# Up products of an MLP by pairs of weight blocks, in seven block products instead of eight, with the square of the norm's rate applied on the down products

## The chip, the cores and the metric

The kernel runs on one core of one Trainium2 chip. The metric is the device time of one execution in microseconds. Matrix products run on TensorE (PE in the profile; the loading of weights is the row PEld), element-wise work on VectorE (DVE), ScalarE (ACT) and GpSimd (POOL), and transfers are issued by SyncE (SP). All of these take their instructions in order from queues of their own and meet at semaphores.

## The reference

Two layers of a streaming encoder over 640 positions (512 of a prompt, 8 x 16 of samples), 1024 features, all in float32. The change concerns the last line of a layer:

```python
def trunk_layer(x, ...):
    h = rmsnorm(x, ln1)
    proj = h @ w_in                                  # all branches
    ...
    x = x + mix @ w_o
    h2 = rmsnorm(x, ln2)
    x = x + jnp.square(jax.nn.relu(h2 @ w_up)) @ w_down   # w_up 1024 x 4096, w_down 4096 x 1024
```

rmsnorm multiplies each position by a rate 1/sqrt(mean(x^2) + 1e-6) and each feature by a weight. The rate is positive, so relu(rate * y)^2 = rate^2 * relu(y)^2, and a factor for each position can be applied before or after any product over features.

## The kernel before

Activations lie feature by feature: `x` is 128 partitions x 8 chunks x 640 positions. Every float32 matrix operand is kept as two float32r parts, hi (a copy on ACT, rounded) and lo (the difference, on DVE), made by `split`. A product takes three matmuls for each chunk of 128 features: hi times hi, hi times lo, lo times hi (`three`). The 640 positions go in two halves of 320 columns, so one block of 128 output features (`gemm`) is 2 halves x 8 chunks x 3 = 48 matmuls of 128x128 by 128x320. Its result is a `pair`: one PSUM tile of two banks, one for each half (pg_up, pg_dn, pg_wo in the profile); there are two such pairs in turn. There are also two single banks `c` and two `d`.

Weights come in blocks of 128x1024 in the order of a list (`Feed`): `load` issues the transfer of one block (three buffers raw), `ahead` splits the next block into whi and wlo (two buffers of each) and loads another, and `take` hands out the split block and asks for the one after it. The splits are set ahead of other work by a priority; a scheduler orders ACT, DVE, POOL and SP by priorities, and the order of PE is the order of the source (`manual_schedule`).

The MLP of a layer (`mlp`) has 32 up blocks and 32 down blocks, in four groups b of eight. All eight up blocks of group 0 come first; then, for each b, two up blocks of the next group, the eight down blocks of b, and the other six up blocks. After an up block, `relu2` takes relu and the rate out of the pair on DVE, squares it to the hi part on ACT and again on POOL, and takes the lo part on DVE: 128x640 each. After a down block DVE adds the pair to `x`. The last eight down blocks are in `residual`, which also sums the squares for the next norm. Ahead of the MLP `residual_raw` makes the products with w_o (pg_wo), adds them to `x` and splits x times the norm's weight into Ah and Al, without the rate; the rate follows beside the first up block. Its last block is taken half by half (`halves=True`): DVE reads the first half of the pair while the second is still to be multiplied.

## Time and profile before

| | |
|---|---|
| median of the runs shown | 2523.02 us (lowest 2522.17) |
| the profiled execution's own time | 2522.23 us |
| its span | 2520.5 us |
| PE busy | 2465.8 us, 98% of the span, 18456 matmuls |
| DVE, ACT, POOL busy | 1300.5, 1024.0, 564.8 us |
| DMA | 104 GB/s in the mean |
| up products, both layers | 3 x 1024 matmuls |
| down products, both layers | 3 x 1024 matmuls |

The page gives busy time by engine, then by forty slices of the span, then groups of instructions with the mean time of one and the idle time ahead of them. The mean of a matmul is from its start to its end; matmuls overlap, so the time from one start to the next is shorter and is read from rows in order of time.

### The profile page before, as it was taken

What the parts mean: (1) busy time and instruction counts of PE and PEld (TensorE: products, weight loads), DVE (VectorE), ACT (ScalarE), POOL (GpSimd) and SP (SyncE); (2) the same over time, 40 slices, a digit from 0 to 9 for tenths busy, and PEclk for the clock granted to TensorE, in tenths of its full rate; (3) what the DMA queues carried; (4) which work ended last, traced back from release to release, by engine and by line L of the source; (5) the groups of instructions that cost most, each with busy time, mean ns of one, the idle gap of its engine ahead of it and who ended that gap; (6) DMA issues with size and microseconds to landing.
All of it is one profiled execution on the core that took longest, in us unless ns stands there. A gap on an engine that the chain in (4) does not pass through costs nothing. (4 is left out here: it accounts for less than half of the span.)

```text
span 2520.5 us, 45083 instructions
## 1 busy us (share of the span) xinstructions
PE 2465.8 (98%) x18456; PEld 2386.6 (95%) x18456; DVE 1300.5 (52%) x2686; ACT 1024.0 (41%) x1968; POOL 564.8 (22%) x638
## 2 busy tenths in 40 slices
PE   8999999999999999999999999999999999999998
PEld 7999999998999999999999999999989999999997
DVE  6656776537555433333445677664275653333333
ACT  5766666533223212122346666774332222122122
POOL 0234433211222201011213333331112221011012
PEclk9999999999999999999999999999999999999999
DMA  5224333336532222222233333333565222222221
GB/s 176 91 96 129 95 95 94 118 118 243 166 102 67 76 76 76 76 76 76 76 98 111 100 95 95 100 120 112 156 213 149 90 70 76 76 74 75 74 73 67
DMA packets 124494, 261.28 MB, mean 104 GB/s; under 512 B 17233, under 2 KB 57073, under 8 KB 124289
## 3 DMA queue, kind: packets, MB, share of 16 engines
q1 hardware_dynamic: 123968, 257.10, 32.2%
q8 instruction: 145, 2.38, 0.4%
q0 software_dynamic: 320, 1.31, 0.2%
q14 instruction: 61, 0.49, 0.1%
HBM read 218.22 MB, written 40.15 MB: 103 GB/s over the span
## 5 line engine op out<-in xcount | busy, mean ns | idle before, releaser
L133 ACT ACTIVATE whi<-raw 128x1024 fp32r<-128x1024 f32 x304 | 321.8, 1059 | 1022.0 <-issue 359.9
L134 DVE TENSOR_TENSOR wlo<-raw,whi 128x1024 fp32r<-128x1024 f32 x304 | 397.3, 1307 | 164.0 <-ACT whi L133 155.6
L80 PE MATMUL pg_dn<-gl,whi 128*128 128x320 f32 x1024 | 316.6, 309 | 2.1 <-DVE gl L1111 2.1
L80 PE MATMUL pg_up<-Ah,whi 128*128 128x320 f32 x1024 | 317.1, 310 | 0.0
L80 PE MATMUL pg_dn<-gh,whi 128*128 128x320 f32 x1024 | 316.7, 309 | 0.0
L80 PE MATMUL pg_up<-Ah,wlo 128*128 128x320 f32 x1024 | 316.4, 309 | 0.0
L80 PE MATMUL pg_dn<-gh,wlo 128*128 128x320 f32 x1024 | 316.4, 309 | 0.0
L80 PE MATMUL pg_up<-Al,whi 128*128 128x320 f32 x1024 | 316.4, 309 | 0.0
L80 PE MATMUL pg_g<-Ah,whi 128*128 128x320 f32 x896 | 289.6, 323 | 0.0
L80 PE MATMUL pg_g<-Ah,wlo 128*128 128x320 f32 x896 | 276.8, 309 | 0.0
L80 PE MATMUL pg_g<-Al,whi 128*128 128x320 f32 x896 | 276.4, 308 | 0.0
L1110 POOL TENSOR_TENSOR r<-r 128x640 f32<-128x640 f32 x64 | 101.8, 1591 | 684.8 <-ACT gh L1109 684.8
L80 PE MATMUL pg_p<-Ah,whi 128*128 128x320 f32 x768 | 252.8, 329 | 0.0
L80 PE MATMUL pg_p<-Al,whi 128*128 128x320 f32 x768 | 237.4, 309 | 0.4 <-DVE Al L134 0.4
L80 PE MATMUL pg_p<-Ah,wlo 128*128 128x320 f32 x768 | 237.6, 309 | 0.0
L80 PEld LDWEIGHTS pg_dn<-gl,whi 128*128 128x128 f32 x1024 | 192.2, 188 | 2.6 <-DVE gl L1111 2.6
L80 PEld LDWEIGHTS pg_up<-Ah,whi 128*128 128x128 f32 x1024 | 192.2, 188 | 0.0
L80 PEld LDWEIGHTS pg_up<-Al,whi 128*128 128x128 f32 x1024 | 192.2, 188 | 0.0
L80 PEld LDWEIGHTS pg_dn<-gh,whi 128*128 128x128 f32 x1024 | 192.2, 188 | 0.0
L80 PEld LDWEIGHTS pg_dn<-gh,wlo 128*128 128x128 f32 x1024 | 192.2, 188 | 0.0
L80 PEld LDWEIGHTS pg_up<-Ah,wlo 128*128 128x128 f32 x1024 | 192.2, 188 | 0.0
L80 PEld LDWEIGHTS pg_g<-Ah,whi 128*128 128x128 f32 x896 | 168.6, 188 | 7.8 <-issue 3.5
(689 smaller groups left out, 5386.8 us busy)
## 6 DMA issues: line engine op xcount, KB each, us to landing
raw<-in_wblk SPq DMA_DIRECT2D x304, 512.0 KB, 3.6
gd<-sg SPq DMA_DIRECT2D x56, 320.0 KB, 3.5
rg<-gd SPq DMA_DIRECT2D x44, 320.0 KB, 3.3
S<-in_sdelta SPq DMA_DIRECT2D x16, 512.0 KB, 6.1
out<-S SPq DMA_DIRECT2D x16, 512.0 KB, 3.6
gr<-rowd SPq DMA_DIRECT2D x16, 320.0 KB, 4.9
er<-rowd SPq DMA_DIRECT2D x16, 320.0 KB, 4.0
ond<-osb SPq DMA_DIRECT2D x16, 320.0 KB, 2.2
```

The source lines that it names most:

```text
L80: nc.tensor.matmul(out, lhsT=lhsT, rhs=rhs, start=start, stop=stop, **kw)
L133: nc.scalar.activation(dst_hi, src, AF.Copy)
L134: nc.vector.tensor_tensor(dst_lo, src, dst_hi.bitcast(F32), op=ALU.subtract)
L1110: nc.gpsimd.tensor_tensor(r[:], r[:], r[:], op=ALU.mult)
```

## The change

In each layer the first four up blocks stay as they were, except that relu is taken on ACT and the rate is left out. The other 28 are done two at a time by `seven(b, m)`. The pair's weights are cut into four parts of 128x512 (two halves of the input features times two blocks), the activations into four of 4 chunks x 320 positions. Winograd's form of Strassen's scheme takes seven products of such parts, of 12 matmuls each, instead of eight. In the order of PE they are called P1 to P7 here:

| | result | weights | activations |
|---|---|---|---|
| P1 | Z, new | first half of block m | Ah, Al, first features, first positions |
| P2 | Y, new | second half of block m | second features, first positions |
| P3 | Z, added | t1, first half | S2 |
| P4 | X, new | t1, second half | S1 |
| P5 | Z, added | t2, first half | S3 (written over a quarter of Ah, Al) |
| P6 | X, added | second half of block m+1 | S4 |
| P7 | Z, added | t2, second half | second features, second positions |

Z and X are the two banks of one pair (pg_zx), Y is a single bank `c`. Between products ACT copies what Z holds after P1 (z1) and after P3 (z2) and X after P4 (x5); DVE adds Y and z1, Z and x5 (after P5), X and z2 (after P6). Relu, the two squares and the lo part follow from these sums, all on ACT and DVE. The weight sums t1 and t2 are made on DVE from the raw blocks, and each of the weights wa (block m), wb (t1), wc (half of t2, half of block m+1) and wd (half of t2) is split on ACT and DVE into the two buffers of whi and wlo in turn. S1 to S4 are made once for each layer, from x times the norm's weight, on ACT and DVE beside the four single up blocks. A down block's sum is now two instructions on DVE: the pair times the square of the rate, and the addition to `x`.

```diff
         def parts(self, pl):
-            raw = self.raw.pop(0)
+            self.last = self.raw.pop(0)
+            return self.of(pl, self.last[:])
+        def of(self, pl, *src):
...
             hi = pl.tile([P, D], F32R, tag="whi", bufs=2, name="whi")
             lo = pl.tile([P, D], F32R, tag="wlo", bufs=2, name="wlo")
+            at = 0
             with tc.high_priority(offset=AHEAD):
-                split(hi[:], lo[:], raw[:])
+                for v in src:
+                    n = v.shape[-1]
+                    split(hi[:, at:at + n], lo[:, at:at + n], v)
+                    at += n
             return hi, lo
...
-            nc.scalar.activation(u, pr[:, 0:HT], AF.Copy)
+            nc.scalar.activation(u, pr[:, 0:HT], AF.Copy if self.power == 1 else AF.Square)
...
         def add(xs, ps, dst, first):
-            nc.vector.tensor_tensor(xs, ps[:, :, 0:HT], xs, op=ALU.add)
+            plus(xs, ps, dst)
             nrm.add(dst, xs, first, nc.vector if dst == 1 else nc.gpsimd)
...
+            def flat(nm, rows):
+                return pl.tile([P, rows, HT], F32, tag="r", bufs=3, name=f"{nm}{l}")
+            def squares(r, hi, lo, eng):
+                nc.scalar.activation(hi, r, AF.Square)
+                if eng is None:
+                    nc.scalar.activation(r, r, AF.Square)
+                else:
+                    eng.tensor_tensor(r, r, r, op=ALU.mult)
+                nc.vector.tensor_tensor(lo, r, hi.bitcast(F32), op=ALU.subtract)
             def relu2(ps, hi, lo):
-                r = pl.tile([P, 2, HT], F32, tag="r", bufs=3, name=f"r{l}")
-                nc.vector.scalar_tensor_tensor(r[:], ps[:, :, 0:HT], 0.0, v2(nrm.r[:]), op0=ALU.max, op1=ALU.mult)
-                nc.scalar.activation(hi, r[:], AF.Square)
-                nc.gpsimd.tensor_tensor(r[:], r[:], r[:], op=ALU.mult)
-                nc.vector.tensor_tensor(lo, r[:], hi.bitcast(F32), op=ALU.subtract)
+                r = flat("r", 2)
+                nc.scalar.activation(r[:], ps[:, :, 0:HT], AF.Relu)
+                squares(r[:], hi, lo, nc.gpsimd)
             def up(b, ms):
                 for m in ms:
                     hi, lo = (v2(v[:, m % 2, :]) for v in dst(b, m))
                     run(gemm(l, WB_UP + b * KC + m, Ah, Al, f"up{l}{b}{m}", lambda ps: relu2(ps, hi, lo)), rates)
-            up(0, range(KC))
+            A = {(k, a): [v[:, 4 * k:4 * k + 4, half[a]] for v in (Ah, Al)] for k in range(2) for a in range(2)}
+            S = {i: [psum_pool.tile([P, 4, HT], F32R, name=f"S{i}{t}{l}")[:] for t in "hl"] for i in (1, 2, 4)}
+            S[3] = A[0, 1]
+            tmp = [pl.tile([P, 4, HT], F32, tag=t, name=f"s{i}{l}")[:] for i, t in enumerate(("gh", "gl", "gh", "gl", "gh"))]
+            def scaled(d, k, a):
+                for i in range(4):
+                    c = nrm.c0 + 4 * k + i
+                    nc.scalar.activation(d[:, i, :], x[:, 4 * k + i, half[a]], AF.Copy, scale=col[:, c:c + 1])
+            def plus(d, s0, s1):
+                nc.vector.tensor_tensor(d, s0, s1, op=ALU.add)
+            q, p, sm, u, v = tmp
+            up(0, range(2))
+            scaled(q, 1, 1)
+            scaled(p, 0, 1)
+            plus(sm, p, q)
+            split(*S[1], sm)
+            up(0, range(2, 3))
+            scaled(u, 0, 0)
+            plus(sm, sm, u)
+            split(*S[2], sm)
+            plus(p, p, u)
+            scaled(v, 1, 0)
+            plus(sm, sm, v)
+            split(*S[4], sm)
+            up(0, range(3, 4))
+            split(*S[3], p)
+            stacks.pop().close()
+            pw = ExitStack()
+            stacks.append(pw)
+            pt = pw.enter_context(phase(f"nt{l}", side="right"))
+            def seven(b, m):
+                gh, gl = dst(b, m)
+                wa = feed.take(l, WB_UP + b * KC + m, ahead=False)
+                B = {}
+                for i, raw in enumerate((feed.last, feed.raw.pop(0))):
+                    B[0, i], B[1, i] = raw[:, 0:512], raw[:, 512:1024]
+                s1, s2 = (pt.tile([P, 2, 512], F32, tag=t, name=f"{t}{l}{b}{m}") for t in ("t1", "t2"))
+                with tc.high_priority(offset=AHEAD):
+                    sub = lambda d, s0, y: nc.vector.tensor_tensor(d, s0, y, op=ALU.subtract)
+                    neg = lambda d, s0, y: nc.vector.scalar_tensor_tensor(d, s0, -1.0, y, op0=ALU.mult, op1=ALU.subtract)
+                    sub(s1[:, 1, :], B[0, 0], B[0, 1])
+                    neg(s1[:, 0, :], s1[:, 1, :], B[1, 1])
+                wb = feed.of(wp, s1[:].rearrange("p a b -> p (a b)"))
+                zx, y = pair(f"zx{l}{b}{m}"), bank("c", f"y{l}{b}{m}")
+                Z, X, Y = zx[:, 0, 0:HT], zx[:, 1, 0:HT], y[:, 0:HT]
+                def product(ps, w, i, act, first):
+                    hi, lo = (t[:, 512 * i:512 * i + 512].rearrange("p (k c) -> p k c", k=4) for t in w)
+                    ah, al = act
+                    for k in range(4):
+                        for j, (wt, act) in enumerate(((hi, ah), (hi, al), (lo, ah))):
+                            nc.tensor.matmul(ps, lhsT=wt[:, k, :], rhs=act[:, k, :], start=first and k + j == 0,
+                                             stop=k == 3 and j == 2, skip_group_check=True)
+                def copy(t, ps):
+                    c = pt.tile([P, HT], F32, tag=t, name=f"{t}{l}{b}{m}")
+                    nc.scalar.activation(c[:], ps, AF.Copy)
+                    return c[:]
+                def add(d, ps, c):
+                    nc.vector.tensor_tensor(d, ps, c, op=ALU.add)
+                product(Z, wa, 0, A[0, 0], True)
+                z1 = copy("z1", Z)
+                product(Y, wa, 1, A[1, 0], True)
+                r0, r1 = flat("ra", 2), flat("rb", 2)
+                add(r0[:, 0, :], Y, z1)
+                with tc.high_priority(offset=AHEAD):
+                    sub(s2[:, 0, :], B[1, 1], B[0, 1])
+                    neg(s2[:, 1, :], s1[:, 0, :], B[1, 0])
+                wc = feed.of(wp, s2[:, 0, :], B[1, 1])
+                feed.load()
+                product(Z, wb, 0, S[2], False)
+                z2 = copy("z2", Z)
+                product(X, wb, 1, S[1], True)
+                x5 = copy("x5", X)
+                wd = feed.of(wp, s2[:, 1, :])
+                product(Z, wc, 0, S[3], False)
+                with tc.high_priority(offset=AHEAD):
+                    add(r1[:, 1, :], Z, x5)
+                product(X, wc, 1, S[4], False)
+                add(r0[:, 1, :], X, z2)
+                nc.scalar.activation(r0[:], r0[:], AF.Relu)
+                squares(r0[:], gh[:, :, half[0]], gl[:, :, half[0]], None)
+                feed.ahead()
+                product(Z, wd, 0, A[1, 1], False)
+                nc.scalar.activation(r1[:, 0, :], Z, AF.Relu, scale=-1.0)
+                nc.scalar.activation(r1[:, 1, :], r1[:, 1, :], AF.Relu, scale=-1.0)
+                squares(r1[:], gh[:, :, half[1]], gl[:, :, half[1]], None)
+            def plus_products(xs, ps, a):
+                t = flat("t", 2)
+                rate = v2(nrm.r[:]) if a is None else rep(nrm.r[:, half[a]], 1, 2)
+                nc.vector.tensor_tensor(t[:], ps[:, :, 0:HT], rate, op=ALU.mult)
+                nc.vector.tensor_tensor(xs, t[:], xs, op=ALU.add)
+            seven(0, 4)
+            seven(0, 6)
             for b in range(FF // D):
                 if b + 1 < FF // D:
-                    up(b + 1, range(2))
+                    seven(b + 1, 0)
                 gh, gl = Chunks(tiles, b, 0), Chunks(tiles, b, 1)
                 if b + 1 == FF // D:
                     last = l + 1 == DEPTH
-                    es.close()
-                    es = ExitStack()
+                    stacks.pop().close()
+                    stacks.pop().close()
+                    es = stacks.pop()
                     pn = es.enter_context(phase(f"na{l}", side="right"))
-                    return es.close, residual(l, WB_DN + b * KC, gh, gl, f"dn{l}", Norm(pn, 32 if last else 16 * (l + 1), f"a{l}", last))
+                    return es.close, residual(l, WB_DN + b * KC, gh, gl, f"dn{l}", Norm(pn, 32 if last else 16 * (l + 1), f"a{l}", last), plus_products)
                 for m in range(KC):
-                    def add(ps):
-                        nc.vector.tensor_tensor(v2(x[:, m, :]), ps[:, :, 0:HT], v2(x[:, m, :]), op=ALU.add)
-                    run(gemm(l, WB_DN + b * KC + m, gh, gl, f"dn{l}{b}{m}", add))
-                up(b + 1, range(2, KC))
+                    run(gemm(l, WB_DN + b * KC + m, gh, gl, f"dn{l}{b}{m}", lambda ps: plus_products(v2(x[:, m, :]), ps, None)))
+                for m in (2, 4, 6):
+                    seven(b + 1, m)
```

Three places in the order of the built programs follow. The first is TensorE in layer 0, group 1, blocks 4 and 5. Before, at the border of the two halves of block 4 (what is awaited stands behind a row; Activation_49 and DVE_49 are the semaphores that ACT and DVE count up, PE_49 that of PE):

```order
L80 MATMUL pg_up014_10252<-Ah_98,whi_10184 128x320
L80 MATMUL pg_up014_10252<-Al_99,whi_10184 128x320
L80 MATMUL pg_up014_10252<-Ah_98,wlo_10185 128x320
L80 MATMUL pg_up014_10252<-Ah_98,whi_10184 128x320
L80 MATMUL pg_up014_10252<-Al_99,whi_10184 128x320
L80 MATMUL pg_up014_10252<-Ah_98,wlo_10185 128x320
```

TensorE now, the last rows of P3 and the first of P4:

```order
L1198 MATMUL pg_zx014_10375<-S2h0_9044,whi_10371 128x320
L1198 MATMUL pg_zx014_10375<-S2l0_9045,whi_10371 128x320
L1198 MATMUL pg_zx014_10375<-S2h0_9044,wlo_10372 128x320
L1198 MATMUL pg_zx014_10375<-S1h0_9042,whi_10371 128x320 [waits Activation_49]
L1198 MATMUL pg_zx014_10375<-S1l0_9043,whi_10371 128x320
```

Where P3 wrote Z and P4 begins X, in the other bank, a wait has come in. TensorE now, the last rows of P5 and the first of P6:

```order
L1198 MATMUL pg_zx014_10375<-Ah_98,whi_10408 128x320
L1198 MATMUL pg_zx014_10375<-Al_99,whi_10408 128x320
L1198 MATMUL pg_zx014_10375<-Ah_98,wlo_10409 128x320
L1198 MATMUL pg_zx014_10375<-S4h0_9046,whi_10408 128x320 [waits DVE_49]
L1198 MATMUL pg_zx014_10375<-S4l0_9047,whi_10408 128x320
```

The halves of an up block follow each other without a wait, while a product on one bank of pg_zx stands behind a wait for ACT (by its count, the copy z2) or for DVE (by its count, the sum of Z and x5). P5 in the same way waits for the copy x5 and P7 for the sum of X and z2, in all 28 pairs.

The second place is ScalarE. Before, at up blocks of group 0 (the row of two kinds in turn is the same in all groups):

```order
L133 ACTIVATE whi_9248<-raw_0_92_9130 128x1024 [waits DMAHW4_49,PE_49,Activation_49]
L1109 ACTIVATE gh002_9186<-r0_9243 128x640 [waits DVE_49]
L133 ACTIVATE whi_9310<-raw_0_93_9192 128x1024 [waits DMAHW5_49,PE_49,Activation_49]
L1109 ACTIVATE gh002_9186<-r0_9303 128x640 [waits DVE_49]
L133 ACTIVATE whi_9370<-raw_0_94_9252 128x1024 [waits DMAHW6_49,PE_49,Activation_49]
L1109 ACTIVATE gh004_9308<-r0_9365 128x640 [waits DVE_49]
```

ScalarE now, at the pair of blocks 4 and 5 of group 1 (z1, z2 and x5 are the copies, whi_10408 is wc, whi_10444 wd):

```order
L1203 ACTIVATE z1014_10389<-pg_zx014_10375 128x320 [waits PE_49]
L1123 ACTIVATE gh012_10229<-rb0_10268 128x2x320 [waits Activation_49]
L1125 ACTIVATE rb0_10268<-rb0_10268 128x640 [waits Activation_49]
L133 ACTIVATE whi_10408<-t2014_10368 128x512 [waits DVE_49,PE_49]
L133 ACTIVATE whi_10408<-raw_0_101_10278 128x512 [waits DMAHW5_49]
L1203 ACTIVATE z2014_10428<-pg_zx014_10375 128x320 [waits PE_49]
L133 ACTIVATE whi_10444<-t2014_10368 128x512 [waits DVE_49,PE_49]
L1203 ACTIVATE x5014_10442<-pg_zx014_10375 128x320 [waits PE_49]
```

Two kinds of rows in turn have become a list in which copies out of PSUM stand between splits of weights.

The third place is ScalarE at the first pair of layer 0 (blocks 4 and 5 of group 0), where the rows before are those shown above, and where now S2, S3 and S4 are still being made:

```order
L133 ACTIVATE S2h0_9044<-s20_9050 128x1280 [waits DVE_49]
L133 ACTIVATE whi_9363<-t1004_9359 128x1024 [waits PE_49]
L1132 ACTIVATE r0_9346<-pg_up003_9297 128x640 [waits PE_49,Pool_49]
L133 ACTIVATE Ah_98<-s10_9049 128x4x320 [waits DVE_49]
L1123 ACTIVATE gh002_9214<-r0_9346 128x640 [waits Activation_49]
L133 ACTIVATE whi_9400<-t2004_9360 128x512 [waits PE_49]
L133 ACTIVATE whi_9400<-raw_0_93_9220 128x512 [waits DMAHW5_49]
L133 ACTIVATE S4h0_9046<-s20_9050 128x1280 [waits DVE_49]
L1203 ACTIVATE z1004_9381<-pg_zx004_9367 128x320
```

Here the copy z1, for which P3 waits, stands behind wc (whi_9400), whose buffer is free after P2, and behind the hi part of S4. Layer 1 has the same order.

More of the change, by code (lines that the diff above doesn't have):

```diff
@@ L280, in encoder, with __init__ @@
     class Norm:
-        def __init__(self, pl, c0, nm, final=False, whole=False):
-            self.pl, self.c0, self.nm, self.final = pl, c0, nm, final
-            self.r = pl.tile([P, NT], F32, tag="rate", name=f"rate{nm}") if whole else None
+        def __init__(self, pl, c0, nm, final=False, whole=None, power=1):
+            self.pl, self.c0, self.nm, self.final, self.power = pl, c0, nm, final, power
+            self.r = whole.tile([P, NT], F32, tag="rate", name=f"rate{nm}") if whole else None
             self.acc = pl.tile([P, 2, HT], F32, tag="acc", name=f"acc{nm}")
@@ L833, in heads @@
             else:
-                nrm = Norm(pf, 0, "a", whole=True)
+                nrm = Norm(pf, 0, "a", whole=pf)
                 Rh = pf.tile([P, KC, NT], F32R, name="Rh")
@@ L1050, in merge, with residual @@
                         run(gemm(l, WB_PA + m, Ah, Al, f"pa{l}{m}", pa))
-            es = ExitStack()
-            nrm = Norm(es.enter_context(phase(f"nb{l}", side="right")), 8 * (2 * l + 1), f"b{l}", whole=True)
-            return es, nrm, residual_raw(l, WB_WO, Bh, Bl, f"wo{l}", nrm)
-    def residual(l, b0, ah, al, nm, nrm):
+            stacks = [ExitStack() for _ in range(3)]
+            pr, ps, pn = (es.enter_context(phase(f"n{nm}{l}", side="right")) for es, nm in zip(stacks, "rsb"))
+            nrm = Norm(pn, 8 * (2 * l + 1), f"b{l}", whole=pr, power=2)
+            return stacks, ps, nrm, residual_raw(l, WB_WO, Bh, Bl, f"wo{l}", nrm)
+    def residual(l, b0, ah, al, nm, nrm, plus):
         def add(xs, ps, dst, first):
-            nc.vector.tensor_tensor(xs, ps[:, :, 0:HT], xs, op=ALU.add)
+            plus(xs, ps, dst)
             nrm.add(dst, xs, first, nc.vector if dst == 1 else nc.gpsimd)
@@ L1094, in residual_raw, with mlp @@
         return rates()
-    def mlp(l, es, nrm, rates):
+    def mlp(l, stacks, psum_pool, nrm, rates):
         with phase(f"mlp{l}", 5) as pl:
@@ L1124, in mlp @@
                     last = l + 1 == DEPTH
-                    es.close()
-                    es = ExitStack()
+                    stacks.pop().close()
+                    stacks.pop().close()
+                    es = stacks.pop()
                     pn = es.enter_context(phase(f"na{l}", side="right"))
-                    return es.close, residual(l, WB_DN + b * KC, gh, gl, f"dn{l}", Norm(pn, 32 if last else 16 * (l + 1), f"a{l}", last))
+                    return es.close, residual(l, WB_DN + b * KC, gh, gl, f"dn{l}", Norm(pn, 32 if last else 16 * (l + 1), f"a{l}", last), plus_products)
                 for m in range(KC):
-                    def add(ps):
-                        nc.vector.tensor_tensor(v2(x[:, m, :]), ps[:, :, 0:HT], v2(x[:, m, :]), op=ALU.add)
-                    run(gemm(l, WB_DN + b * KC + m, gh, gl, f"dn{l}{b}{m}", add))
-                up(b + 1, range(2, KC))
+                    run(gemm(l, WB_DN + b * KC + m, gh, gl, f"dn{l}{b}{m}", lambda ps: plus_products(v2(x[:, m, :]), ps, None)))
+                for m in (2, 4, 6):
+                    seven(b + 1, m)
     ctx.enter_context(tc.manual_schedule(engines={mybir.EngineType.PE}))
```

## The prediction

> **What bounds the kernel now.** I read the page's shares of engines first, then the windows of the MLP, then the groups by shape, then the rows in order of time around one up block, and last the waits of TensorE.
>
> ```profile
> span 2520.5 us, 45083 instructions
> PE 2465.8 (98%) x18456; PEld 2386.6 (95%) x18456; DVE 1300.5 (52%) x2686; ACT 1024.0 (41%) x1968; POOL 564.8 (22%) x638
> ```
>
> The windows of layer 0 (columns: length, then busy us and instructions of PE, PEld, DVE, ACT, POOL, then granted clock, DMA share, GB/s), with the start of the kernel and the products with w_o for comparison:
>
> ```profile
> 20.00:30.00 10.00, 8.25 (x38) 7.85 (x39) 6.08 (x14) 4.06 (x6) 0.33 (x1) 0.66 0.23 71
> 730.00:800.00 70.00, 67.48 (x457) 66.73 (x456) 42.68 (x40) 21.26 (x28) 17.59 (x9) 1.00 0.25 76
> 800.00:820.00 20.00, 19.05 (x136) 18.79 (x135) 8.43 (x14) 6.04 (x9) 3.29 (x3) 1.00 0.17 53
> 870.00:1230.00 360.00, 358.94 (x2447) 358.68 (x2446) 125.29 (x129) 74.27 (x82) 42.27 (x27) 1.00 0.25 77
> ```
>
> In the MLP (last row) TensorE has 2447 matmuls in 360 us and no idle time; DVE is busy for 35%, ACT for 21%, transfers for 25%. So a matmul fewer is worth what lies between two starts, and any wait that TensorE meets there is paid in full.
>
> Rows of time at the end of one up block and the start of the next:
>
> ```profile
> 818.52 0.82 DVE L1108 SCALAR_TENSOR_TENSOR r<-pg_up,rateb 128x640 f32<-128x640 f32 x1 [2.89 <-PE pg_up L80]
> ...
> 825.07 0.31 PE L80 MATMUL pg_up<-Al,whi 128*128 128x320 f32 x1
> 825.22 0.31 PE L80 MATMUL pg_up<-Ah,wlo 128*128 128x320 f32 x1
> ...
> 825.46 1.06 ACT L133 ACTIVATE whi<-raw 128x1024 fp32r<-128x1024 f32 x1 [5.34 <-issue]
> ...
> 825.56 0.82 DVE L1108 SCALAR_TENSOR_TENSOR r<-pg_up,rateb 128x640 f32<-128x640 f32 x1 [2.85 <-PE pg_up L80]
> ```
>
> A matmul lasts 0.31 us but the next starts 0.15 us later: from one DVE row to the next are 7.04 us, and a block has 48 matmuls, so 0.1467 us is the price of one. Two delays are read here as well. DVE begins on the result 0.34 us after the block's last matmul began (825.22 to 825.56). ACT overwrites a whi buffer 0.24 us after that same start; the matmul before it was the last to read the buffer.
>
> **Part 1, the matmuls removed.** A pair of blocks has 7 x 12 = 84 matmuls instead of 96: 12 x 0.1467 = 1.76 us. There are 14 pairs in each layer, 28 in all: 28 x 1.76 = -49.3 us. If nothing waited, a pair would take 12.32 us in place of 14.08.
>
> **Part 2, the waits inside a pair.** P4, P5, P6 and P7 each begin with a wait on an instruction that reads the other bank, and that instruction itself waits for the end of the product just before. TensorE has nothing to do in between, since its order is fixed. The trace has one place of this form: the last pg_wo block, half by half, where DVE reads the first half before TensorE begins the second.
>
> ```profile
> 794.09 2.19 DVE L134 TENSOR_TENSOR Al<-hwo,Ah 128x640 fp32r<-128x640 f32 x1
> ...
> 794.80 0.31 PE L80 MATMUL pg_wo<-Bh,wlo 128*128 128x320 f32 x1
> 796.20 0.48 DVE L1076 TENSOR_TENSOR x<-pg_wo,x 128x320 f32<-128x320 f32 x1
> ...
> 796.73 0.41 PE L80 MATMUL pg_wo<-Bh,whi 128*128 128x320 f32 x1 [1.62 <-DVE x L1076]
> ...
> 796.99 0.30 PE L80 MATMUL pg_wo<-Bl,whi 128*128 128x320 f32 x1
> ...
> 797.12 0.31 PE L80 MATMUL pg_wo<-Bh,wlo 128*128 128x320 f32 x1
> ...
> 800.40 1.06 ACT L133 ACTIVATE whi<-raw 128x1024 fp32r<-128x1024 f32 x1 [2.80 <-PE pg_wo L80]
> ...
> 801.37 0.45 ACT L292 ACTIVATE sqb<-x 128x320 f32<-128x320 f32 x1
> ```
>
> TensorE starts 0.05 us after DVE has ended (796.68 to 796.73), and the next start comes 0.26 us later instead of 0.15: a restart costs 0.11 us. DVE was late here for a reason of its own (the 2.19 us row); without it the wait would be 0.34 + 0.48 + 0.05. The last two rows show that a queued ACT instruction starts 0.09 us before the one ahead has ended.
>
> Durations by shape (busy us and mean ns of one):
>
> ```profile
> L133 ACT ACTIVATE whi<-raw 128x1024 fp32r<-128x1024 f32 x304 | 321.8, 1059 | 1022.0 <-issue 359.9 <-PE pg_dn L80 256.3 <-PE pg_up L80 79.1
> ...
> L134 DVE TENSOR_TENSOR wlo<-raw,whi 128x1024 fp32r<-128x1024 f32 x304 | 397.3, 1307 | 164.0 <-ACT whi L133 155.6
> ...
> L1110 POOL TENSOR_TENSOR r<-r 128x640 f32<-128x640 f32 x64 | 101.8, 1591 | 684.8 <-ACT gh L1109 684.8
> ...
> L1109 ACT ACTIVATE gh<-r 128x640 fp32r<-128x640 f32 x64 | 46.9, 732 | 0.0
> ...
> L1131 DVE TENSOR_TENSOR x<-pg_dn,x 128x640 f32<-128x640 f32 x48 | 39.6, 825 | 221.3 <-PE pg_dn L80 221.3
> ...
> L821 ACT ACTIVATE sg<-pg_g 128x640 f32<-128x640 f32 x56 | 39.2, 700 | 13.4 <-DMA gd<-sg 12.9
> ...
> L461 ACT ACTIVATE cb<-pg_p 128x320 f32<-128x320 f32 x48 | 20.1, 419 | 0.0
> ...
> L343 ACT ACTIVATE ha<-x,col 128x320 f32<-128x320 f32 x32 | 16.2, 550 | 3.7 <-DMA out<-ha 3.3 <-DVE Al L134 0.4
> ```
>
> The copies z1, z2 and x5 are 128x320 out of PSUM on ACT, as cb<-pg_p is: 0.42 us. The sums are 128x320 on DVE, as the row at 796.20 is: 0.48 us. A 128x512 split is not shown; half of 128x1024 is 0.53 us and the whole 1.06, and on the line through the 320-wide (0.45, the row at 801.37) and the 1024-wide row it would be 0.62, which I take. Each wait is counted from the start of the last matmul of the product ahead, less the 0.147 us that the next would have come later anyhow:
>
> - P4 waits for z2: 0.34 + 0.42 + 0.05 - 0.15 = 0.66.
> - P5 waits for x5, which stands on ACT behind the hi split of wd, and that waits for P4's last reads of wb's buffer: 0.24 + 0.62 - 0.09 + 0.42 + 0.05 - 0.15 = 1.09.
> - P6 waits for DVE's sum of Z and x5: 0.34 + 0.48 + 0.05 - 0.15 = 0.72.
> - P7 waits for DVE's sum of X and z2: 0.72.
>
> These are 3.19 us, and four restarts 0.44: 3.63 us in a pair, against 1.76 saved. The net is +1.87, a pair takes 15.95 us, and 28 x 1.87 = +52.4 us. From below, without restarts and with x5 ahead of the split, it is 2.76 - 1.76 = +1.0; from above, with half a microsecond more for a queue that is late once, +2.4: 28 to 66 us.
>
> P1 and P3 are taken at nothing in a steady pair. P2 covers the copy z1 (0.34 + 0.42 against 1.76). For P1 of the next pair the whole split wa must follow P5 (the wc buffer) and stand ready after P6 and P7, which are 1.76 us each and now have waits beside them: 1.06 on ACT and 1.31 on DVE, of which the two overlap only in part, leave some 0.4 us. If that cover goes, each pair pays for it; that is the second rival.
>
> What hides the rest: in a pair ACT has 3 copies, splits of 1024, 1024, 3 x 512, relu and squares of two halves, about 9.7 us of 16, and DVE, by the rows above with half of 1.31 for each 512-wide one, about 10.6 of 16. Both have more than before in a pair but neither is full, and nothing on TensorE waits for gh and gl until their group's down blocks. POOL loses its squares there. The two raw transfers of a pair keep their time of 14 to 16 us, twice what a block's split had. A down block's sum has one more 0.83 us row on DVE beside 7.04 us of products, which only the last one doesn't hide.
>
> **Part 3, the first pair of each layer.** Here z1 stands on ACT behind the making of S1 to S4. From the end of the second single up block until z1 is done, ACT has the hi split of that stretch's weights twice (2 x 1.06), relu and square twice (2 x 1.43), eight scaled copies (8 x 0.55), three splits of 1280 columns (about 1.28 each by the same line), wc (2 x 0.62) and z1 (0.42): 14.9 us, less some 1.5 for the overlaps (0.09 each), plus about 0.8 for DVE's sums between them: 14.2. TensorE needs it after 72 matmuls, 10.56 us. The wait at P3 is about 3.7 us, twice: +7.4 (0 to 12).
>
> That idle time has its own consequence. The only idle time of that order of size among long runs of matmuls is at the start:
>
> ```profile
> PE pg_gf L80 <- ACT whi L133: 2.6, 1, 2.6
> PE pg_wo L80 <- DVE x L1076: 3.2, 2, 1.6
> PE pg_dn L80 <- DVE gl L1111: 2.1, 2, 1.1
> ```
>
> ```profile
> 18.43 0.31 PE L80 MATMUL pg_gf<-Rh,wlo 128*128 128x320 f32 x1
> ...
> 21.39 0.63 PE L80 MATMUL pg_gf<-Rh,whi 128*128 128x320 f32 x1 [2.65 <-ACT whi L133]
> ...
> 27.08 0.47 PE L80 MATMUL pg_gf<-Rh,whi 128*128 128x320 f32 x1
> 27.35 0.46 PE L80 MATMUL pg_gf<-Rl,whi 128*128 128x320 f32 x1
> 27.61 0.34 PE L80 MATMUL pg_gf<-Rh,wlo 128*128 128x320 f32 x1
> ```
>
> After 2.65 us of idle time the starts are 0.27 us apart, until 27.6 us, and the window 20:30 has a clock of 0.66. Its 38 matmuls would take 5.6 us and took 8.6 less 0.4 of another wait: about 2.7 us lost. After the 1.6 us wait in pg_wo the clock stayed 1.00. A 3.7 us wait may bring the loss in both layers or in neither; I take it once: +2.7 (0 to 5.4).
>
> [...]
>
> **Part 4, the ends.** The last down block's sum stands ahead of the final norm, and has a second DVE instruction: +0.8. The waits of pg_dn for gl (2.1 us in both layers) come from a last up block whose lo part is late; POOL's 1.6 us square is gone there, and I take -1.2 (-2.1 to 0).
>
> **Sum.** -49.3 + 101.6 (28 x 3.63) + 7.4 + 2.7 + 0.8 - 1.2 = +62.0 us against the profiled execution's 2522.2: 2584 us. The median is 2523.02, and the forecast is 2.4% above it. The bounds of the terms: lowest 28 + 0 + 0 + 0.8 - 2.1 = +27, highest 66 + 12 + 5.4 + 0.8 = +84, so 2549 to 2606.
>
> **The rivals.**
>
> The other side: *the border waits are cheap*. The place is P4 to P7. If TensorE begins while the other bank is read, the four cost nothing and the time is 2522.2 - 49.3 + 9.7 = 2483 us, no slower than before. It decides where a border costs under (49.3 - 9.7) / 112 = 0.35 us in the mean. For it: the two banks hold different results, and nothing computed by P4 needs z2. Against: the 1.62 us row shows TensorE waiting in just such a case, and the built program has the wait. Even a copy that lasted nothing would leave 0.34 + 0.05 - 0.15 + 0.11 = 0.35. Chance 0.05. [...] A part of the waits (z2 and x5 hidden, the two sums paid: 2 x 0.83 a pair) would give 2522.2 - 49.3 + 46.5 + 9.7 = 2529; chance 0.05.
>
> *The queues pile up.* At the turn of a pair, ACT has relu, two squares and wa's split, and DVE two lo parts, wa's lo split and the next sums. If a square or a lo part (0.73 to 0.83) comes ahead of what TensorE waits for, twice in a pair, it costs about 1.5 us: 28 x 1.5 = 42, 2584 + 42 = 2626. For it: the margin of 0.4 us at P1. Against: the splits and the P6 sum are put ahead by priority, and both engines have 5 us free in a pair. Chance 0.13.
>
> *The clock halves within pairs.* TensorE is now idle for 3.2 of 16 us. If this brings one loss of 2.7 us in each pair: 28 x 2.7 = 76, 2660. For it: the row of 2.65 us. Against: 1.62 us left the clock at 1.00, and no wait in a steady pair is above 1.1. Chance 0.07. [...]
>
> **How the numbers follow.** The forecast has 0.70, and the rivals 0.05, 0.05, 0.13 and 0.07. The range takes in the forecast's bounds and the queues up to 2630: 2549 to 2630; what is left out are the two cheap cases, the clock and a little of the queues, about 2 in 10. A measurement of this kernel tells about 2% from no change: 2472.6 and 2573.5. The forecast's own 2549 to 2606 lies to three quarters above 2573.5, so slower has 0.70 x 0.75 + 0.13 + 0.07 = 0.72; the rest of it and the cheap cases are within 2%, 0.26; faster by over 2% would need more than all matmuls saved at no cost, 0.02.
>
> **What would show it.** Right: TensorE has 336 matmuls fewer; four rows of idle time in a pair, of about 0.6 to 0.8 us and one of 1.1, ended by z2, x5 and the two sums; starts of Z's first products 16 us apart; one wait of 3 to 4 us for z1 in each layer; the clock at 1.00 in the pairs. Wrong: waits below 0.35 us, or pairs 14 us or less apart; a wait at P1 or P3 in each pair; clock below 1.00 in the windows of pairs; or idle time that moved into the down blocks.

## The result, and the profile after

The changed kernel takes 2588.32 us (median, 2585.98 to 2591.85), against 2523.64 us for the kernel before on the same chip: a ratio of 1.0264, with a 95% interval from 1.0247 to 1.028. It is slower by 2.6%; the forecast was 2584 us, 2.4%, in a range from 2549 to 2630.

The first lines of the page after:

```profile
span 2585.7 us, 44993 instructions
PE 2450.6 (95%) x18120; PEld 2340.2 (91%) x18120; DVE 1477.5 (57%) x2982; ACT 1213.4 (47%) x2324; POOL 476.9 (18%) x582
```

TensorE has the 336 matmuls fewer (18456 to 18120) and is busy for 15 us less, but the span is 65 us longer. TensorE's share falls from 98% to 95%, and the waits of TensorE (awaited instruction: us in total, times, longest) say for what:

```profile
PE pg_zx L1198 <- ACT x L1203: 25.1, 28, 0.9
PE pg_zx L1198 <- ACT z L1203: 21.2, 30, 3.2
PE pg_zx L1198 <- DVE rb L1207: 18.2, 28, 0.7
PE pg_zx L1198 <- DVE ra L1207: 16.4, 28, 0.6
...
PE pg_dn L80 <- DVE gl L1128: 0.4, 2, 0.2
```

The four lines on pg_zx are new. x is the copy x5 (P5 waits), z is z2 in 28 pairs and z1 twice, rb is the sum of Z and x5 (P6), ra that of X and z2 (P7). Rows in order of time through one steady pair, with the start of P5 in the pair before for the period (rows left out are marked by dots):

```profile
985.54 0.41 PE L1198 MATMUL pg_zx<-Ah,whi 128*128 128x320 f32 x1 [0.90 <-ACT x L1203]
...
998.17 0.44 ACT L1203 ACTIVATE z<-pg_zx 128x320 f32<-128x320 f32 x1 [0.65 <-PE pg_zx L1198]
...
998.66 0.41 PE L1198 MATMUL pg_zx<-S1h,whi 128*128 128x320 f32 x1 [0.53 <-ACT z L1203]
...
1000.58 0.63 ACT L133 ACTIVATE whi<-t 128x512 fp32r<-128x512 f32 x1 [1.97 <-PE pg_zx L1198]
1001.11 0.42 ACT L1203 ACTIVATE x<-pg_zx 128x320 f32<-128x320 f32 x1
...
1001.59 0.41 PE L1198 MATMUL pg_zx<-Ah,whi 128*128 128x320 f32 x1 [0.90 <-ACT x L1203]
...
1003.70 0.49 DVE L1207 TENSOR_TENSOR rb<-pg_zx,x 128x320 f32<-128x320 f32 x1 [1.77 <-PE pg_zx L1198]
...
1004.25 0.42 PE L1198 MATMUL pg_zx<-S4h,whi 128*128 128x320 f32 x1 [0.64 <-DVE rb L1207]
...
1006.22 1.06 ACT L133 ACTIVATE whi<-raw 128x1024 fp32r<-128x1024 f32 x1 [1.52 <-PE pg_zx L1198]
1006.32 0.49 DVE L1207 TENSOR_TENSOR ra<-pg_zx,z 128x320 f32<-128x320 f32 x1 [2.13 <-PE pg_zx L1198]
...
1006.87 0.42 PE L1198 MATMUL pg_zx<-Ah,whi 128*128 128x320 f32 x1 [0.58 <-DVE ra L1207]
...
1007.31 1.23 DVE L134 TENSOR_TENSOR wlo<-raw,whi 128x1024 fp32r<-128x1024 f32 x1 [0.50 <-ACT whi L133]
...
1009.02 0.31 PE L80 MATMUL pg_dn<-gh,wlo 128*128 128x320 f32 x1
```

Each PE row with a bracket is the first matmul of P4, P5, P6 or P7, and just ahead of it ends the copy or sum that reads the other bank. The last two rows, the lo split of the next weights and the first matmul that reads it, are taken up further below. From P5 to P5 of the next pair (985.54 to 1001.59) are 16.05 us, where 14.08 were taken before and 12.32 would be without waits.

The windows at the first pair of each layer and at steady pairs (last columns: granted clock, DMA share, GB/s):

```profile
840.00:850.00 10.00, 6.42 (x31) 5.76 (x32) 9.07 (x12) 3.49 (x7) 1.43 (x1) 0.83 0.17 52
1000.00:1030.00 30.00, 27.88 (x187) 27.09 (x186) 11.26 (x13) 9.57 (x14) 0.00 (x0) 1.00 0.28 88
2120.00:2130.00 10.00, 7.47 (x45) 6.69 (x46) 8.41 (x12) 2.26 (x6) 0.00 (x0) 1.00 0.19 54
```

The clock is 1.00 in the steady pairs. It fell in layer 0 at the first pair (0.50 from 842.43 to 845.85 us) and not in layer 1, though the wait for z1 was 3.21 us in both.

To compare kernels below I use the stretch of one MLP, from the start of its first pg_up matmul to that of its last pg_dn matmul in the trace, since the rest of the kernel, in which no run changed more than the last sum, differs by some microseconds from one profiled execution to the next (between the two MLPs 784 to 791 us). That difference goes with the granted clock: by the clock records of the traces it was at 0.50 there for 3 x 3.4 us in the kernel before, the change and x5dve (789.3 to 791.1 us), and not at all in banks, early and halves2 (783.9 to 784.7); over the whole executions the mean granted clock was 0.993 to 0.994 in the first three and 0.995 to 0.996 in the others.

| kernel | time, us | kernel before beside it | ratio (95%) | MLP of layer 0, of layer 1, us |
|---|---|---|---|---|
| before | | | | 457.0, 456.9 |
| the change | 2588.32 | 2523.64 | 1.0264 (1.0247 to 1.028) | 488.9, 487.5 |
| banks | 2495.73 | 2521.37 | 0.9902 (0.9884 to 0.992) | 444.5, 444.3 |
| x5dve | 2581.66 | 2521.37 | 1.0241 (1.0226 to 1.0257) | 485.7, 484.8 |
| z1first | 2587.22 | 2521.37 | 1.0259 (1.0242 to 1.0276) | 492.2, 487.2 |
| early | 2579.38 | 2522.66 | 1.0223 (1.0206 to 1.0241) | 486.0, 485.9 |
| halves | 2607.67 | 2521.37 | 1.0346 (1.033 to 1.0361) | 500.1, 500.2 |
| rateonly | 2524.17 | 2522.66 | 1.0011 (1.0 to 1.0022) | 457.7, 457.7 |
| halves2 | 2575.02 | 2522.66 | 1.0205 (1.019 to 1.022) | 483.4, 483.4 |
| best | 2480.76 | 2522.66 | 0.9837 (0.9818 to 0.9856) | 437.7, 437.6 |
| best2 | 2476.37 | 2520.25 | 0.9824 (0.9806 to 0.9843) | 434.1, 434.5 |

Of the 65 us by which the span grew, 31.9 + 30.6 = 62.5 lie in the two MLPs.

### The profile page after: what moved, and what is told of

Read it like the earlier page. It is cut to its first block, busy times and chain, and to the rows that moved or that the text cites. A ratio compares the mean times of both kernels' runs of the same rounds, so it can differ in the third digit from the quotient of the medians.

```text
span 2585.7 us, 44993 instructions
## 1 busy us (share of the span) xinstructions
PE 2450.6 (95%) x18120; PEld 2340.2 (91%) x18120; DVE 1477.5 (57%) x2982; ACT 1213.4 (47%) x2324; POOL 476.9 (18%) x582
## 5 line engine op out<-in xcount | busy, mean ns | idle before, releaser
L133 ACT ACTIVATE whi<-raw 128x1024 fp32r<-128x1024 f32 (+1 forms) x304 | 309.0, 1018 | 686.1 <-PE pg_dn L80 256.6
L134 DVE TENSOR_TENSOR wlo<-raw,whi 128x1024 fp32r<-128x1024 f32 (+1 forms) x304 | 383.5, 1263 | 170.1 <-ACT whi L133 167.9
L80 PEld LDWEIGHTS pg_g<-Al,whi 128*128 128x128 f32 x896 | 168.7, 188 | 1.5
L1241 DVE TENSOR_TENSOR t<-pg_dn,rateb 128x640 f32<-128x640 f32 x64 | 52.7, 824 | 205.0 <-PE pg_dn L80 205.0
L80 PEld LDWEIGHTS pg_g<-Ah,wlo 128*128 128x128 f32 x896 | 168.2, 188 | 0.0
L479 DVE SCALAR_TENSOR_TENSOR yb<-cb,cw,yb 128x664 f32<-128x664 f32 x144 | 138.0, 959 | 27.4 <-ACT yb L477 25.7
L80 PEld LDWEIGHTS pg_p<-Ah,whi 128*128 128x128 f32 x768 | 145.2, 189 | 6.7 <-issue 2.4
L1198 PE MATMUL pg_zx<-Ah,whi 128*128 128x320 f32 x336 | 109.6, 326 | 41.5 <-ACT x L1203 25.1
```

The lines of the kernel that those rows point to most:

```text
L80: nc.tensor.matmul(out, lhsT=lhsT, rhs=rhs, start=start, stop=stop, **kw)
L133: nc.scalar.activation(dst_hi, src, AF.Copy)
L134: nc.vector.tensor_tensor(dst_lo, src, dst_hi.bitcast(F32), op=ALU.subtract)
L479: nc.vector.scalar_tensor_tensor(yb[:, 0:CY], cb[:, j:j + CY], cw[:, c, j:j + 1], yb[:, 0:CY], op0=ALU.mult, op1=ALU.add)
L1198: nc.tensor.matmul(ps, lhsT=wt[:, k, :], rhs=act[:, k, :], start=first and k + j == 0, stop=k == 3 and j == 2, skip_group_check=True)
L1241: nc.vector.tensor_tensor(t[:], ps[:, :, 0:HT], rate, op=ALU.mult)
```

## The experiments

The theory: the change loses its gain because P4 to P7 wait for readers of a bank that they do not write, at 3.6 us a pair. Its rivals were that the border costs nothing and the sums, copies and splits are to blame, that ACT's and DVE's queues are, and that the clock is.

### banks: Z and X in tiles of their own

```diff
-                zx, y = pair(f"zx{l}{b}{m}"), bank("c", f"y{l}{b}{m}")
-                Z, X, Y = zx[:, 0, 0:HT], zx[:, 1, 0:HT], y[:, 0:HT]
+                z, xx, y = bank("d", f"z{l}{b}{m}"), pair(f"x{l}{b}{m}"), bank("c", f"y{l}{b}{m}")
+                Z, X, Y = z[:, 0:HT], xx[:, 0, 0:HT], y[:, 0:HT]
```

> Z and X in PSUM tiles of their own, one bank each, instead of the two banks of one pair; the products, their order and the copies are those of the change. My theory (P4 to P7 wait only because Z and X share a tile, each wait lasting from the end of a product to the end of a copy or a sum): P4 to P7 start without idle time and the four waits go from 74.5 us (25.1 + 14.8 + 18.2 + 16.4) to under 5. The idle time counts from a matmul's end, 0.16 us after the next could have started, and a restart costs 0.11, so a pair loses 2.66 + 4 x 0.27 = 3.74 us and the time falls by 28 x 3.74 = 105 us, from 2588 to about 2483 (2475 to 2492). Rival, the queues: a pair of 12.3 us needs about 9.7 us of ACT and 10.6 of DVE, so waits for splits come up at P1 or P3 of each pair, 1 to 2 us: 2511 to 2540. Rival, contention: ACT and DVE read a bank beside matmuls on another; if that slows either, copies of 0.42 us or matmul pitches of 0.147 us become longer.

It takes 2495.73 us, 93 less than the change and 1% less than the kernel before, but more than the expected 2475 to 2492. Waits of TensorE in the pairs (ps_z is Z):

```profile
PE ps_z L1198 <- ACT z L1203: 6.4, 2, 3.2
...
PE ps_z L1198 <- DVE wlo L134: 5.4, 20, 0.4
...
PE pg_dn L80 <- DVE wlo L134: 2.1, 8, 0.3
```

The four waits of each pair are gone; nothing was taken away but the shared tile. So the cause is settled: the border, not the arithmetic around the products. The copies and sums that now run beside matmuls on another bank last as long as before:

```profile
L1203 ACT ACTIVATE x<-pg_x 128x320 f32<-128x320 f32 x28 | 11.8, 421 | 0.0
...
L1207 DVE TENSOR_TENSOR ra<-pg_x,z 128x320 f32<-128x320 f32 x28 | 13.7, 491 | 20.2 <-PE pg_x L1198 20.2
```

(0.419 and 0.492 us in the change), and the starts of matmuls in a steady pair stay 0.147 us apart, so the rival of contention is out as well. In the MLPs 87.6 of the expected 105 us are gained, and 17 are missing. Most of that is the queues' rival, small: 20 times P1's third matmul, the first that reads the lo part of wa, waits for it, and 8 times the same happens at the down block that follows a pair. Such a matmul starts 0.57 us after the one ahead and the next 0.25 us later: 0.57 + 0.25 - 2 x 0.147 = 0.53 us, and 28 x 0.53 = 15. The rest fits the clock, which fell here after the wait for z1 (3.2 us, as in the change) in both layers and not in one: the 336 matmuls on S2 take 106.9 us in all, where 0.309 us each would be 103.8, and at 0.468 us for one at the lower clock (the change's longest) some 19 of them were slow; in the change, with 105.8 us, it is some 12, the P3 of one layer.

### z1first: the copy z1 ahead on ACT

```diff
-                z1 = copy("z1", Z)
+                with tc.high_priority(offset=2 * AHEAD):
+                    z1 = copy("z1", Z)
```

> Only the order of ACT changes: the copy z1 is put ahead, so that at the first pair of each layer it no longer stands behind wc and the splits of S3 and S4. My theory (the wait at P3 is a place in ACT's list, and the low clock after it in layer 0 follows from the idle time): both waits of 3.2 us go, with the clock's loss of about 1.4 us in layer 0, and the clock stays at 1.00 around 840 us: 2588 - 2 x 3.5 - 1.4 = 2580 (2576 to 2584). Rival: ACT's list as a whole is late, and the wait moves to P5 (S3, wc) or P6 (S4) of the same pair: 2586 to 2590.

The theory fell here. The time stays (2587.22 us): the MLP of layer 1, where the clock kept 1.00, is 0.3 us shorter, and that of layer 0 is even 3.3 us longer. The rows at the first pair of layer 0, then the windows:

```profile
843.07 0.41 PE L1198 MATMUL pg_zx<-S1h,whi 128*128 128x320 f32 x1 [1.77 <-ACT z L1203]
...
846.83 0.64 PE L1198 MATMUL pg_zx<-Ah,whi 128*128 128x320 f32 x1 [0.78 <-ACT x L1203]
...
847.97 0.64 PE L1198 MATMUL pg_zx<-Al,whi 128*128 128x320 f32 x1 [0.50 <-DVE Al L134]
```

```profile
840.00:850.00 10.00, 6.95 (x29) 5.94 (x29) 10.00 (x12) 3.97 (x7) 2.02 (x1) 0.69 0.16 52
850.00:860.00 10.00, 8.76 (x32) 7.96 (x32) 2.33 (x4) 3.47 (x5) 0.00 (x0) 0.50 0.13 27
```

P3 no longer waits, but z2 is late in its place and then the lo part of S3 (Al) on DVE, which is busy for all of 840 to 850. The list of work for S1 to S4 was late as a whole, on both engines, which is the rival, though the waits moved to P4 and to P5's second matmul. And the clock, once down, stayed at 0.50 through the pair: from 843.8 to 860.8 us matmuls start 0.27 us apart instead of 0.147.

### early: S1, S2 and S4 made sooner

```diff
-            up(0, range(2))
+            up(0, range(1))
             scaled(q, 1, 1)
...
-            up(0, range(2, 3))
             scaled(u, 0, 0)
...
             split(*S[4], sm)
-            up(0, range(3, 4))
+            up(0, range(1, 4))
             split(*S[3], p)
```

> The kernel of the change with the making of S1, S2 and S4 put after the first single up block of a layer instead of between the second and the fourth; the pairs are untouched. Theory, formed after the run z1first, where the wait only moved on to z2 and to the lo part of S3 and the clock fell for longer: at the first pair ACT and DVE as a whole are late with S2 to S4, so only earlier work helps. Both waits of 3.2 us at P3 go with their restarts, and the 1.3 us of low clock in layer 0: 2588 - 2 x 3.5 - 1.3 = 2580 (2577 to 2583). Rival: the work is only shifted onto the single up blocks, whose relu then comes late for TensorE: 2586 or more.

2579.38 us is what was expected, but by the stage only half of it is earned: the MLPs are 2.9 and 1.6 us shorter, where 4.8 and 3.5 were expected, and the rest of the difference lies where nothing was changed (4.7 us between the MLPs, where the clock was at 0.50 for 3 x 3.4 us in the change's execution and not at all in this one). That the total came out as forecast is luck.

```profile
PE pg_zx L1197 <- ACT z L1202: 18.0, 30, 1.7
```

The two waits for z1 went from 3.2 to 1.6 us each (18.0 less the 14.8 of z2), and the clock stayed at 1.00 (in all six windows of 10 us from 830 to 860 and from 2100 to 2130). What still stands ahead of z1 on ACT:

```profile
836.39 1.28 ACT L133 ACTIVATE S4h<-s 128x1280 fp32r<-128x1280 f32 x1 [3.87 <-DVE s L1152]
...
841.03 0.42 ACT L1202 ACTIVATE z<-pg_zx 128x320 f32<-128x320 f32 x1
```

From the split of S4 to z1 ACT is busy, and that split had waited 3.87 us for a sum on DVE. So the lateness of the work for S1 to S4 is shown as Part 3's cause for half of the wait. That DVE has its share in the other half is read from this row and was not tried by itself.

### x5dve: the copy x5 on DVE

```diff
-                x5 = copy("x5", X)
+                x5 = pt.tile([P, HT], F32, tag="x5", name=f"x5{l}{b}{m}")[:]
+                with tc.high_priority(offset=2 * AHEAD):
+                    nc.vector.tensor_copy(x5, X)
```

> The copy x5 is taken on DVE instead of ACT, so that it doesn't stand behind the hi split of wd; all else is that of the change. My theory (P5's wait of 0.90 us is longer than P4's 0.53 by the 0.62 us split ahead of the copy): the wait falls to about 0.34 + 0.48 + 0.05 - 0.31 = 0.56 us, 0.34 less in 28 pairs: 2588 - 9.5 = 2578 (2575 to 2582). Rival: DVE, with 0.5 us more in each pair, has the sums of P6 and P7 later by as much: 2586 to 2592.

```profile
PE pg_zx L1198 <- DVE x L1224: 19.4, 28, 1.4
PE pg_zx L1198 <- DVE ra L1207: 18.9, 28, 0.7
PE pg_zx L1198 <- DVE rb L1207: 16.3, 28, 0.6
```

2581.66 us is at the upper end of what was expected. P5's waits fall from 25.1 to 19.4 us in total (in a steady pair from 0.90 to 0.65 us, where 0.56 was expected), P6's from 18.2 to 16.3, and P7's grow from 16.4 to 18.9: net -5.1, and the MLPs are 3.2 and 2.7 us shorter. The split ahead of x5 was a part of P5's wait, and P7's growth gives a third of it back. The rival is right on P7 alone: P6 did not become later.

### halves: the border by itself, on DVE

```diff
-            def relu2(ps, hi, lo):
-                r = pl.tile([P, 2, HT], F32, tag="r", bufs=3, name=f"r{l}")
-                nc.vector.scalar_tensor_tensor(r[:], ps[:, :, 0:HT], 0.0, v2(nrm.r[:]), op0=ALU.max, op1=ALU.mult)
+            def relu2(ps, a, hi, lo):
+                if a == 0:
+                    rs[0] = pl.tile([P, 2, HT], F32, tag="r", bufs=3, name=f"r{l}")
+                r = rs[0]
+                nc.vector.scalar_tensor_tensor(r[:, a, :], ps[:, a, 0:HT], 0.0, nrm.r[:, half[a]], op0=ALU.max, op1=ALU.mult)
+                if a == 0:
+                    return
...
-                    run(gemm(l, WB_UP + b * KC + m, Ah, Al, f"up{l}{b}{m}", lambda ps: relu2(ps, hi, lo)), rates)
+                    run(gemm(l, WB_UP + b * KC + m, Ah, Al, f"up{l}{b}{m}", lambda ps, a: relu2(ps, a, hi, lo), halves=True), rates)
```

> The kernel before with one edit: DVE takes relu and rate of an up block in two instructions, one for each half, so that TensorE must wait in the middle of each of the 64 up blocks for the read of the first half, while it would write the other bank. No matmul is removed and the rate stays on the up products. It measures the border by itself. My theory: each border costs 0.34 + 0.48 + 0.05 - 0.15 + 0.11 = 0.83 us, 64 x 0.83 = +53: 2576 (2570 to 2582). Rival (such a border costs nothing, and the change is slower for its copies, sums and splits): 2520 to 2530.

2607.67 us: the border is dear, but 86 us is far over 53. TensorE's waits, then rows at one border:

```profile
PE pg_up L80 <- DVE r L1112: 69.6, 64, 1.2
```

```profile
818.83 0.82 DVE L1117 TENSOR_TENSOR gl<-r,gh 128x640 fp32r<-128x640 f32 x1 [1.15 <-POOL r L1116]
819.57 0.48 DVE L1112 SCALAR_TENSOR_TENSOR r<-pg_up,rateb 128x320 f32<-128x320 f32 x1
...
820.11 0.42 PE L80 MATMUL pg_up<-Ah,whi 128*128 128x320 f32 x1 [1.12 <-DVE r L1112]
```

On DVE the lo part of the block before stands ahead, and that waits for POOL's square. DVE's read of the half begins 0.55 us later than 0.34 us after the last matmul's start (818.68), which the estimate took, and 64 x 0.55 = 35 is about what the estimate lacks (86 - 53 = 33). The estimate left out what was queued.

### rateonly and halves2: the other half of the change, and the border again

rateonly keeps the relu on ACT and the square of the rate on the down products, and drops the seven products with the making of S1 to S4:

```diff
-            seven(0, 4)
-            seven(0, 6)
+            up(0, range(4, KC))
...
-                    seven(b + 1, 0)
+                    up(b + 1, range(2))
...
-                for m in (2, 4, 6):
-                    seven(b + 1, m)
+                up(b + 1, range(2, KC))
```

> The change without the seven products: all up blocks single with eight, relu on ACT, the square of the rate on the down products. Theory: the rate's move costs the last sum's 0.8 us and saves the waits of pg_dn for gl, 2.1 to 0.4 us: 2520 to 2522 where the kernel before is at 2521. Rival: the two DVE instructions of each down block or relu's place on ACT cost more than they seem: 2526 or more.

halves2 is rateonly with relu by halves on ACT (and `halves=True` as in halves):

```diff
-                nc.scalar.activation(r[:], ps[:, :, 0:HT], AF.Relu)
+                nc.scalar.activation(r[:, a, :], ps[:, a, 0:HT], AF.Relu)
+                if a == 0:
+                    return
```

> The kernel rateonly with relu taken by ACT in two instructions, one for each half of an up block, so that TensorE waits in the middle of all 64 single blocks. It repeats the run halves, where the lo part of the block before, which waits for POOL's square, stood ahead of the first half's instruction on DVE and made the border 1.42 us instead of 0.83; ACT has nothing there. Theory: each border costs 0.34 + 0.42 + 0.05 - 0.15 + 0.11 = 0.77 us, 64 x 0.77 = 49 above rateonly: about 2571 (2566 to 2576). Rival (a border alone costs little, it was DVE's queue): under 2540.

The rate's move costs 0.7 us in each MLP (2524.17 us, ratio 1.0011, where 2520 to 2522 was expected), so next to nothing of the 65 us comes from it. The waits for gl did not fall:

```profile
PE pg_dn L80 <- DVE gl L1128: 2.7, 2, 1.3
```

rateonly still has POOL's squares in every block, and the change has none in its pairs. So the fall to 0.4 us in the change comes with the pairs, whose squares are on ACT, and not with the rate's move. halves2 takes 50.9 us more than rateonly, 49 expected:

```profile
PE pg_up L80 <- ACT r L1136: 34.1, 64, 0.6
```

That is 0.53 us of idle time in the mean, the same as at P4; with the end of the matmul (0.31 - 0.147) and the restart (0.11) 0.80 us a border, 64 x 0.80 = 51. The price of a border holds without any of the seven products about it.

### best and best2: what the scheme is worth

best is banks and early together, with the split of the next pair's wa in two halves of 512:

```diff
-            return self.of(pl, self.last[:])
+            return self.of(pl, *([self.last[:, 0:512], self.last[:, 512:1024]] if self.fine else [self.last[:]]))
...
+                feed.fine = True
                 feed.ahead()
+                feed.fine = False
                 product(Z, wd, 0, A[1, 1], False)
```

> Three edits together: Z and X in tiles of their own (as in banks), S1, S2 and S4 made early (as in early), and the split of the next pair's wa, or of the next down block, in two halves of 512, so that its first half is ready sooner. In banks 20 waits for the lo part of wa and 8 of down blocks for their first lo part, about 0.27 us each and as much again for the end of a matmul and the restart, cost some 15 us. Theory: 2496 - 15 - 2 x 3.5 - 3.4 (the low clock after the wait for z1, both layers) = 2471 (2466 to 2478), 50 below the kernel before: the 49 us of removed matmuls in full. Rival: with pairs of 12.3 us the halves of splits, each with its own fixed cost, make DVE late elsewhere: 2480 to 2490.

2480.76 us, 10 more than expected and within the rival's range, but not for the rival's reason: the waits for wlo are gone. In steady pairs a small one is left that the view of waits does not list; it shows in the rows:

```profile
860.43 0.49 DVE L1207 TENSOR_TENSOR ra<-pg_x,z 128x320 f32<-128x320 f32 x1 [0.59 <-PE pg_x L1198]
...
873.08 0.49 DVE L1207 TENSOR_TENSOR ra<-pg_x,z 128x320 f32<-128x320 f32 x1 [0.86 <-PE pg_x L1198]
```

```profile
1052.53 0.72 ACT L1124 ACTIVATE gh<-rb 128x640 fp32r<-128x640 f32 x1
1053.16 0.42 ACT L1203 ACTIVATE z<-ps_z 128x320 f32<-128x320 f32 x1
```

A pair takes 12.65 us instead of 12.32, and z1 begins just as a square ends: it was held on ACT. best2 adds the edit of z1first:

> The kernel best with one more edit: the copy z1 is put ahead of the squares of the pair before on ACT. In best a steady pair still takes 12.65 us instead of 12.32: P3 starts 0.38 us after P2's last matmul instead of 0.15, and the one after it another 0.11 later, because z1 stands behind two squares of 0.73 us. Theory: 28 x 0.33 = 9.2 us go: 2481 - 9 = 2472 (2468 to 2476). At the first pair of each layer z1 still stands behind one relu and one square, so its wait of 1.6 us stays. Rival: the squares, put back, make the relu or the lo parts late, and other waits come up: 2478 to 2482.

2476.37 us, just above the expected 2468 to 2476. The MLPs are 3.6 and 3.1 us shorter than in best, and in both layers no start between matmuls of a steady pair is late any more. The estimate of 9.2 us counted 28 pairs; z1 was late in the 20 that follow another pair, 20 x 0.34 = 7. What is left are the first pairs and the last up block's lo part:

```profile
PE ps_z L1198 <- ACT z L1203: 3.5, 2, 1.9
...
PE pg_dn L80 <- DVE gl L1129: 1.4, 2, 0.7
```

Against the kernel before the two MLPs save 22.9 + 22.4 = 45.3 of the 49.3 us that the removed matmuls are worth, and the kernel is 1.8% faster (ratio 0.9824, 0.9806 to 0.9843). The same seven products thus cost 65 us when two of their results share a tile and save 26 when these have tiles of their own (banks); they save 44 with the smaller edits of best2 as well.

## Why the prediction was right

- **Part 1, -49.3 us.** Right: 336 matmuls fewer, and best2 comes within 4 us of it.
- **Part 2, +101.6 us.** Right in place, cause and size. By the starts, a steady pair has 16.05 - 12.32 = 3.73 us of waits and restarts, 3.63 forecast. The terms: P5 1.17 (1.20 forecast), P6 0.91 and P7 0.86 (0.83 both), P4 0.79 (0.77). P6's sum starts 0.40 us after P5's last matmul and not 0.34; the rest agrees within 0.04. 28 x 3.73 = 104.4.
- **One step of part 2 was wrong, and cost nothing.** It let the split of wa follow P5. The second half of wc is used by P6, and the row at 1006.22 shows the hi split beginning after P6. In the change P7's own wait hides that: the lo part is done at 1008.54 us and first read at 1009.02, so the cover of some 0.4 us is there, but it is all P7's wait. In banks, where the waits were gone, TensorE stood idle 0.26 us for the lo part.
- **Part 3, +7.4 us.** Right: the wait for z1 was 3.21 us in both layers, with matmul's end and restart 3.5, 3.7 forecast. The text starts its count at the end of the second single up block by a slip: its list and its 72 matmuls belong to the end of the third, and from there to the end of z1 ACT took 13.8 us (828.28 to 842.10) and not 14.2. The step named ACT's list as the cause; z1first shows that DVE's is late too.
- **The clock, +2.7 us.** It happened in one of two layers, as taken, but that was luck: the prediction gave no reason for one rather than two, and in banks the same wait brought it in both. The term was mis-sized. In layer 0, P3's first start to P4's is 3.88 us against 2.56 in layer 1, so 1.3 us. The window 840:850 has a clock of 0.83, which is 3.4 us at 0.50 (842.43 to 845.85) and not the 6.2 of the start (21.39 to 27.6 in the kernel before). Why the same 3.21 us came with the low clock in one layer and without it in the other is not shown; the last section has the windows.
- **Part 4, -0.4 us.** The waits for gl went from 2.1 to 0.4 us (-1.2 forecast, -1.7 measured). From the start of the last pg_dn matmul to the end of the span 15.2 us became 16.7, 1.5 and not 0.8; but over all traces it is 15.2 and 15.8 with the old last sum (before, halves) and 16.0 to 16.7 with the new one, so 0.8 is not refuted.
- **Sum.** 2584 forecast, 2588.32 measured. In the MLPs 62.5 us against 61.2 forecast (62.0 less the 0.8 of the end); part 2 was 2.8 too low, and the clock, z1 and gl together 2.3 too high, so a part of this closeness is luck. 2.7 us lie elsewhere, in stages that the change doesn't touch and in the tail.
- **The rivals.** That the borders are cheap is refuted by the change itself and, apart from it, by halves2. That ACT and DVE read another bank beside matmuls at no cost is right all the same: in banks the copies last 0.421 us and the sums 0.491 (0.419 and 0.492 in the change), with matmuls 0.147 us apart. The queues' rival did not decide in the change and was worth 15 us in banks. The clock in steady pairs stayed at 1.00 (window 1000:1030) with four waits of 0.5 to 0.9 us in 16 us.

## What to carry to other kernels

Where an algorithm saves products but passes results from one bank to the next, count the borders before the products: one that waits for a reader of the neighbouring bank costs the reader's delay, its time and a restart, here 0.8 us or five and a half matmuls, and two of them eat eleven of the twelve matmuls saved. Results that are read at different times want tiles of their own, since in these programs the wait goes by tile and not by bank (74.5 us of such waits in the change, none in banks). And a wait that is taken away uncovers the next one (lo parts, then z1): look at the starts of matmuls, which show gaps that a list of waits leaves out.
